# A diffusion transformer's attention layer: weights split on another engine, output sums held in PSUM, the second norm in another order

## The chip, the cores and the metric

The kernel runs on one core of one Trainium2 chip. The metric is the device time of one execution in microseconds (us). A core has engines that run side by side and wait for each other by semaphores: TensorE (PE; its weight loads are listed as PEld), VectorE (DVE), ScalarE (ACT), GpSimd (POOL) and SyncE (SP, which issues most DMAs). Matmuls write to PSUM, which the kernel uses as eight banks of 128 x 512 floats.

## The reference: two layers on 256 tokens and 256 of context

The input is 256 latent tokens on a grid of 4 x 64 and 256 context tokens, 1024 wide. Layer 0 mixes with a retention scan, layer 1 with neighbourhood attention; each has an MLP with a squared ReLU. Cut to layer 1, where the change lies:

```python
h  = x * (1 + sc1) + sh1                    # modulation; hc likewise from ctx
q, k, v = split(h @ w_in)                   # 32 heads of 32
kc, vc  = split((hc @ w_in)[..., d:])       # keys and values of the context
# a query at (row, column) sees all 4 rows, 16 columns around its own, and the context
s = concat([q . k_band * scale + rpb, q . kc * scale])
o = softmax(s) @ [v_band, vc]
y = o @ w_o
x = layer_norm(a * x + g1 * y)              # first norm of the layer
h = x * (1 + sc2) + sh2
x = layer_norm(a * x + g2 * (relu(h @ w1) ** 2) @ w2)
```

All of it is in float32. "The second norm" in the change's name is the modulated norm between attention and MLP: it is the second of the layer's stages that norm and modulate.

## The kernel before

**Products.** A float32 product is made of three faster ones: each operand is split into a rounded part (hi) and the rest (lo), and hi x hi, hi x lo and lo x hi are summed in PSUM (`mm3`, L179).

**Weights.** All weights come as units of 512 KB, in the order of a list (`specs`). `fetch` (L255) issues a unit's DMA on SP into one of 4 raw tiles and has ACT cast it to hi; the subtraction that makes lo is put on a list, and `lows` (L295) issues so many of these on DVE. hi and lo tiles are rings of 5. `take` (L300) hands units to the matmuls. A raw tile is free again when its lo is made.

**Order.** In the part that the change touches each engine runs its instructions in the order in which the program issues them: a wrapper (`InOrder`, L79) pins the order, and it records every instruction with line 89, so the profile's rows are told apart by the names of their tiles, not by lines. PE, ACT and DVE are pinned through the whole attention layer, POOL only from the tail on.

**The attention loop** (L1832 to L1846) has 14 steps. Work is cut into 16 attention units n: four heads (g = n // 2) and half of the queries (n % 2). Step n does, in program order:

- `turned(n)` (L1675): ACT copies the transposed reciprocals of the sums from the bank `pav` to `rt`;
- `scores(n + 2)` (L1591): matmuls into four banks (`pqk`) from `qT` and `kT`;
- `soften(n + 2)` (L1609): for each of four heads, DVE adds the bias to the scores and takes the minimum in one custom instruction (`s<-pqk,bias`, and `mn`; called a biased sum below), then ACT takes the exponential and its sum; at its end POOL issues the DMA of a later unit's bias;
- side work that keeps TensorE busy: a group's keys K(2) to K(7), queries Q(2), Q(3), four blocks of values V(0) to V(3), or blocks of the output projection (W00, W01, W10: first half of the heads' sums for output half and token tile), set by the table `STEPS` (L1811);
- `flip(n + 1)` (L1649): 16 small and 8 larger transposes of the exponentials (`ppt`), copied out by ACT and DVE as a near part and a far part (`pt`), and the transpose of the reciprocals (`pav<-cst,rr`);
- `attend(n)` (L1680): 16 groups of matmuls into `pav`, a product with `rt` on DVE, and its split into `oTh` (ACT) and `oTl` (DVE);
- `invert(n + 2)` (L1637): the reciprocals of the sums and their widening (`rr`), both on DVE.

The five columns of `STEPS` say how many units are fetched and made low ahead of the scores (early), behind the exponentials (late) and behind the flip (last), and which side work runs ahead of the flip and behind attend.

**The tail** (from L1849) does the last two units' attend, the second half of the output projection (`wo_last`, L1863), the gated residual (`gated`, `add_to`), the layer norm's statistics (`stat`, `moments`), the centring of the halves (`center`, tile `xn`), the transposes of these (`pt<-cst,xn`), the affine modulation and its split (`affine_half`: `hTh`, `hTl`), and the first four blocks of the MLP's first product (`tok_block`: p00, p01, p10, p11, tiles `p1t`; the first digit is the token tile). In the tail, before the change, the weight unit that does not fit in the rings lives in scratch tiles.

Of the kernel before, what the change touches and what calls it, by code (L numbers as in the profile page):

```python
# [17 lines left out]
P = 128  # L18
# [74 lines left out]


class Rows:


    def __init__(self, tiles):
        self.tiles = tiles

    def __getitem__(self, at):
        p, k, cols = at
        return self.tiles[k][p, cols]
# [6 lines left out]
def kernel(  # L110
# [144 lines left out]
    def fetch(n, in_scratch=False):  # L255

        for src, k, ncol in specs[len(units) : len(units) + max(n, 0)]:
            raw = rawp.tile([P, k, ncol], F32, tag="raw", name=nm("raw"))
            sp.dma_start(out=raw[:], in_=src.rearrange("(k p) n -> p k n", p=P))
            if in_scratch:  # L260
                hi, lo = Rows([scr("hi", F32R) for _ in range(k)]), Rows([scr("lo", F32R) for _ in range(k)])
                for i in range(k):
                    act.copy(out=hi[:, i, :], in_=raw[:, i, :])
                    pending.append((lo[:, i, :], raw[:, i, :], hi[:, i, :]))
                units.append((hi, lo))
                continue
            hi = hip.tile([P, k, ncol], F32R, tag="hi", name=nm("hi"))
            lo = lop.tile([P, k, ncol], F32R, tag="lo", name=nm("lo"))
# [1380 lines left out]
    def flip(n):  # L1649
# [30 lines left out]
    def attend(n):  # L1680
# [32 lines left out]
    def wo_first(half, t):  # L1713
# [4 lines left out]
        mmo(wops[half, t], t, (0, 1, 2, 3), wous[half])  # L1718
# [70 lines left out]
    flip(0)  # L1789
# [18 lines left out]
    W00, W01, W10, W11 = [W(half, t) for half in range(2) for t in range(2)]  # L1810
# [16 lines left out]

    def run(fs):
        for f in fs:
            f()  # L1830

    for n, (early, late, last, before, after) in enumerate(STEPS):  # L1832
# [27 lines left out]
    x0, x1 = xn2[:, 0, :], xn2[:, 1, :]  # L1860
    st1 = small(smp, 24, "st1", name="st1", bufs=1).rearrange("p (q s) -> p q s", q=4)

    def wo_last(t, half, cols=slice(0, 512)):  # L1863
        ps = bank("pnw")
        mmo(ps, t, (4, 5, 6, 7), us[half::2], cols)
        return ps

    def settle_last(t, half, ps):
        add_to(t, half, gated(ps, t, half, G1), dve)
        if t == 0:  # L1870
            stat(t, half)
# [13 lines left out]
    pool.on = True  # L1885
# [10 lines left out]
    for half in range(2):  # L1896
        center(0, half, mv0, r0, x0, shift)
    settle_last(1, 0, wo_last(1, 0))
    for q in range(2):
        stat_quarter1(q)  # L1900
# [6 lines left out]
    def affine_half(pts, half, t, on_act):  # L1907
# [5 lines left out]
        return lambda: dve.tensor_sub(out=lo, in0=av_, in1=hi.bitcast(F32))  # L1913

    def tok_block(t, f2):
        ps = bank("p1t")
        for k in range(KC):
            wh, wl = us4[2 * f2 + k // 4]
            mm3(
                ps[:, :256], hs(k, t * P, (t + 1) * P), (wh[:, k % 4, :], wl[:, k % 4, :]),  # L1920
                k == 0, k == KC - 1,
            )
# [26 lines left out]
    fetch(2)  # L1949
# [28 lines left out]
    HS1 = [N_Q, N_V, N_B, N_P0, N_P1, N_OH, N_OL, N_K1]  # L1978
# [153 lines left out]
```

## Time and profile before

| | |
|---|---|
| median of 3 runs (lowest, highest) | 1217.92 us (1217.80, 1218.52) |
| the profiled execution | 1219.88 us |
| its span in the trace | 1218.10 us |
| mean granted TensorE clock | 0.992 |
| attention loop from V(0) to V(3), tail, in the trace | about 865 to 990, 990 to 1032 |

Rows of a timeline give start and duration in us, the engine, the operation with its output and input tiles, how many instructions are drawn together (x), and in brackets the idle time ahead of them with what ended it. Rows of groups give total busy time and mean ns of one instruction, then the idle time ahead of them. Rows of the windows view give a stretch, its length, and each engine's busy time in it, then the granted clock of TensorE. Rows of waits give who waits for whom, us in total, how often, and the longest. Durations of matmuls overlap, so the distance of their starts is what counts.

### The profile page before, as it was taken

What the parts mean: (1) busy time and instruction counts of PE and PEld (TensorE: products, weight loads), DVE (VectorE), ACT (ScalarE), POOL (GpSimd) and SP (SyncE); (2) the same over time, 40 slices, a digit from 0 to 9 for tenths busy, and PEclk for the clock granted to TensorE, in tenths of its full rate; (3) what the DMA queues carried; (4) which work ended last, traced back from release to release, by engine and by line L of the source; (5) the groups of instructions that cost most, each with busy time, mean ns of one, the idle gap of its engine ahead of it and who ended that gap; (6) DMA issues with size and microseconds to landing.
All of it is one profiled execution on the core that took longest, in us unless ns stands there. A gap on an engine that the chain in (4) does not pass through costs nothing.

```text
span 1218.1 us, 18130 instructions
## 1 busy us (share of the span) xinstructions
PE 1189.4 (98%) x7138; PEld 991.0 (81%) x7138; DVE 811.0 (67%) x1277; ACT 479.6 (39%) x818; POOL 167.9 (14%) x190
## 2 busy tenths in 40 slices
PE   9999999999999999999999999999999989999996
PEld 6768888888888888888888888888777767999885
DVE  3686766956788476468866664667465677776445
ACT  3652232222323145232213341246465655565331
POOL 0203301420520240000220000230201000000002
PEclk9999999999999999999999999999999989999998
DMA  9665342584255224347665656636543343665661
GB/s 323 214 225 160 121 137 75 160 303 137 93 158 157 80 79 136 92 128 252 196 214 173 215 190 203 200 100 201 169 124 126 120 133 105 193 204 185 225 191 41
DMA packets 134445, 199.15 MB, mean 163 GB/s; under 512 B 15376, under 2 KB 76872, under 8 KB 134360
## 3 DMA queue, kind: packets, MB, share of 16 engines
q1 hardware_dynamic: 129528, 183.86, 47.5%
q0 software_dynamic: 3584, 11.59, 3.1%
q10 hardware_dynamic: 1248, 2.54, 0.7%
q8 instruction: 56, 0.92, 0.3%
q14 instruction: 29, 0.24, 0.1%
HBM read 189.46 MB, written 10.61 MB: 164 GB/s over the span
## 4 chain that ended last, share of the span: by engine, by line
PE 84%; DVE 7%; ACT 5%; DMA 2%; issue 1%; SPq 0%; DVEq 0%; ACTq 0%
PE p L89 41%; PE pg L89 7%; PE pw L89 7%; PE pq L89 6%; PE pv L89 6%; PE pnv L89 3%; PE pn L89 3%; PE po L89 3%; PE pada L89 2%; DVE lo L89 2%; ACT s L89 2%; PE pS L89 1%; ACT hi L89 1%; PE pnw L89 1%; PE ppt L89 1%
## 5 line engine op out<-in xcount | busy, mean ns | idle before, releaser
L89 DVE TENSOR_TENSOR lo<-raw,hi 128x1024 fp32r<-128x1024 f32 (+1 forms) x235 | 276.9, 1193 | 132.8 <-ACT hi L89 132.1
L89 ACT CAST hi<-raw 128x1024 fp32r<-128x1024 f32 (+1 forms) x235 | 234.4, 1011 | 330.9 <-PE p L89 138.8
L89 PE MATMUL p<-hi,hid 128*128 128x512 f32 (+1 forms) x832 | 242.7, 374 | 0.0
L89 PEld LDWEIGHTS p<-hi,hid 128*128 128x128 f32 x832 | 152.2, 188 | 29.1 <-issue 1.6
L89 PE MATMUL p<-hTh,lo 128*128 128x256 f32 (+1 forms) x512 | 168.7, 330 | 0.8 <-DVE lo L89 0.8
L89 PE MATMUL p<-hTh,hi 128*128 128x256 f32 (+1 forms) x512 | 169.1, 331 | 0.0
L89 PE MATMUL p<-hTl,hi 128*128 128x256 f32 (+1 forms) x512 | 168.7, 330 | 0.0
L89 PE MATMUL p<-lo,hid 128*128 128x512 f32 (+1 forms) x416 | 155.3, 373 | 0.0
L89 POOL TENSOR_TENSOR R<-R,acc 128x512 f32<-128x512 f32 x40 | 68.0, 1711 | 277.7 <-DVE acc L89 277.6
L89 PEld LDWEIGHTS p<-hTh,lo 128*128 128x128 f32 x512 | 97.3, 190 | 9.7 <-DVE lo L89 1.0
L89 PEld LDWEIGHTS p<-hTh,hi 128*128 128x128 f32 x512 | 97.2, 190 | 9.6 <-issue 0.8
L89 PEld LDWEIGHTS p<-hTl,hi 128*128 128x128 f32 x512 | 97.3, 190 | 9.0 <-DVE hTl L89 0.4
L89 DVE SCALAR_TENSOR_TENSOR acc<-rawa,scol,acc 128x1024 f32<-128x1024 f32 x56 | 73.9, 1338 | 41.5 <-DMA rawa<-in_ada_w_dram 41.2
L89 PEld LDWEIGHTS p<-lo,hid 128*128 128x128 f32 x416 | 78.4, 188 | 13.4
L89 DVE SCALAR_TENSOR_TENSOR strips<-rawa,scol,strips 128x512 f32<-128x512 f32 x84 | 71.0, 889 | 0.5 <-DMA rawa<-in_ada_w_dram 0.5
L89 ACT CAST hid<-r 128x256 fp32r<-128x256 f32 (+1 forms) x64 | 32.0, 500 | 82.1 <-DVE r L89 82.1
L89 DVE TENSOR_TENSOR hid<-r,hid 128x256 fp32r<-128x256 f32 (+1 forms) x64 | 34.6, 541 | 32.6 <-ACT hid L89 32.4
L89 ACT ACTIVATE s<-s,mn 128x416 f32<-128x416 f32 x64 | 40.4, 633 | 32.5 <-DVE mn L89 32.0
L89 PE MATMUL pg<-hi,hTh 128*128 128x512 f32 x128 | 51.0, 399 | 0.0
L89 PE MATMUL pw<-hi,oh 128*128 128x512 f32 x128 | 51.0, 398 | 0.0
L89 PE MATMUL pv<-hi,hTh 128*128 128x512 f32 x128 | 50.7, 396 | 0.0
L89 PE MATMUL pw<-hi,ol 128*128 128x512 f32 x128 | 50.3, 393 | 0.0
(213 smaller groups left out, 2190.1 us busy)
## 6 DMA issues: line engine op xcount, KB each, us to landing
raw<-in_mlp_w_dram SPq DMA_DIRECT2D x128, 512.0 KB
rawa<-in_ada_w_dram SPq DMA_DIRECT2D x80, 512.0 KB
raw<-in_ret_w_in_dram SPq DMA_DIRECT2D x46, 512.0 KB
raw<-in_nat_w_in_dram SPq DMA_DIRECT2D x24, 512.0 KB
rawq<-in_ada_w_dram SPq DMA_DIRECT2D x16, 512.0 KB
raw<-in_ret_w_o_dram SPq DMA_DIRECT2D x16, 512.0 KB
rpb_near<-far SPq DMA_DIRECT2D x20, 256.0 KB
bias<-rpb_near POOLq DMA_DIRECT2D x16, 320.0 KB, 3.9
```

The costliest lines, as they stand in the source:

```text
L89: r = f(*args, **kwargs)
```

## The change

- `soften` of a step no longer has weight subtractions ahead of its biased sums: those sums are DVE's first work behind the scores. In steps 1 to 9 the subtractions are issued on POOL (`lows(1, pool)`), 13 of them; POOL is pinned in order from the loop's start. In step 0 one is left on DVE, behind the first sum. From step 10 on, one a step is issued on DVE behind the sums.
- `flip` is cut into `flip_near` and `flip_far`. The copies of the near part now come ahead of the evacuation of K or Q, the far part behind it. `attend` comes ahead of `invert`.
- Q(3) runs at the start of step 9 ahead of K(6), and six units are fetched in that step where there were four.
- A unit may live in an arena slot that is idle at that time (`home`), which takes the place of the scratch tiles.
- W01 and W10 are not read out after the heads' first half: their banks are held from step 12 and 13, and the second half is summed on top in the tail. W11 is made in the tail, in halves of 256 columns, over all heads in one bank each. So three products with the gate and three sums into the residual of 512 columns fall away.
- In the tail `flip(15)` and `turned(15)` come directly behind `attend(14)`, `attend(15)` behind the second output block, the first token tile's norm ahead of the second tile's last output blocks; p01 is cut into three pieces with the second tile's transposes between them, and `tok_part` sums the terms by kind, those with the low part of the activations last, in each half of the chunks. `fold` and POOL's other operations stand in the pinned order.

The core of the diff (the table `STEPS` is cut to two rows):

```diff
-    def fetch(n, in_scratch=False):
+    def fetch(n, home=None):
...
+            if home is None:
+                hi = hip.tile([P, k, ncol], F32R, tag="hi", name=nm("hi"))
+                lo = lop.tile([P, k, ncol], F32R, tag="lo", name=nm("lo"))
+            else:
+                both_ = slot(home, [P, 2, k, ncol], F32R, "unit")
+                hi, lo = both_[:, 0], both_[:, 1]
...
-    def lows(n=100):
+    def lows(n=100, eng=None):
         for lo, raw, hi in pending[:n]:
-            dve.tensor_sub(out=lo, in0=raw, in1=hi.bitcast(F32))
+            (eng or dve).tensor_sub(out=lo, in0=raw, in1=hi.bitcast(F32))
...
-    def soften(n):
+    def soften(n, between=lambda: None):
...
+            if j == 0:
+                between()
...
-    def flip(n):
+    def flip_near(n):
...
+    def flip_far(n):
...
-        (1, 1, 0, [V(0)], []),
+        ((None,), (None,), V(0), ()),
...
-        (0, 0, 1, [W01[0]], [W01[1]]),
+        ((), (), W01, (None,)),
...
+    pool.on = True
+
+    def weights(homes, eng=None):
+        for home in homes:
+            fetch(1, home)
+            if eng:
+                lows(1, eng)
+
+    for n, (early, late, before, last) in enumerate(STEPS):
         turned(n)
-        fetch(early)
-        lows(early)
+        weights(early, pool if n else None)
         scores(n + 2)
-        soften(n + 2)
-        fetch(late)
-        lows(late)
-        run(before)
-        flip(n + 1)
+        soften(n + 2, lambda: lows(0 if n else 1))
+        if n > 9:
+            lows(1)
+        weights(late, pool if n < 10 else None)
+        if n == 9:
+            Q(3)()()
+            weights((None, None), pool)
+            fetch(1)
+        evac = before()
+        flip_near(n + 1)
+        if evac:
+            evac()
+        flip_far(n + 1)
+        attend(n)
         invert(n + 2)
-        fetch(last)
-        attend(n)
-        run(after)
-        lows()
+        if n == 10:
+            wo_add(0, 0)
+        weights(last, pool if n < 10 else None)
...
     turned(n - 1)
-    attend(n - 1)
-    flip(n)
-    fetch(1, True)
-    lows()
+    weights((N_Q, N_B))
+    attend(n - 1, lambda: lows(1))
+    flip_near(n)
+    flip_far(n)
+    turned(n)
+    lows(2)
...
-    settle_last(0, 0, wo_last(0, 0))
-    settle_last(0, 1, wo_last(0, 1))
+    ps = wo_last(bank("pnw"), 0, 0, first=True)
+    add_to(0, 0, gated(ps, 0, 0, G1), dve)
+    stat(0, 0)
+    tmp = gated(wo_last(wops[1, 0], 0, 1), 0, 1, G1)
+    attend(n, lambda: add_to(0, 1, tmp, dve))
+    weights((N_P0, N_P1))
+    stat(0, 1)
     mv0, r0 = moments(0)
-    turned(n)
-    attend(n)
-    W11[0]()
-    fetch(2)
-    W11[1]()
-    lows()
...
+    add_to(1, 0, gated(wo_last(wops[0, 1], 1, 0), 1, 0, G1), dve)
...
+    mmo(ps[0], 1, (0, 1, 2, 3), wous[1], halves[0], last=False)
     pts0 = [mod_pt(x0, half) for half in range(2)]
     lo0 = [affine_half(pts0, half, 0, True) for half in range(2)]
-    ps = [wo_last(1, 1, slice(256 * q, 256 * q + 256)) for q in range(2)]
...
+    mmo(ps[1], 1, (0, 1, 2, 3), wous[1], halves[1], last=False)
```

What the instructions' order makes of it, at three places. DVE in step 1, with K(3) beside it, before the change (`lo` are the weight subtractions, `s` and `mn` the biased sums, `kT` the split of K):

```order
L89 TENSOR_TENSOR oTl_6961<-rt_7193,oTh_6960 128x128
L89 TENSOR_TENSOR lo_7326<-raw_7323,hi_7325 128x1024
L89 TENSOR_TENSOR lo_7331<-raw_7328,hi_7330 128x1024
L89 ISA s_7353,mn_7351<-pqk_7335,bias_6884 128x416
L89 ISA mn_7351 128x1
L89 ISA s_7356,mn_7351<-pqk_7336,bias_6884 128x416
L89 ISA mn_7351 128x1
L89 ISA s_7359,mn_7351<-pqk_7337,bias_6884 128x416
L89 ISA mn_7351 128x1
L89 ISA s_7362,mn_7351<-pqk_7338,bias_6884 128x416
L89 ISA mn_7351 128x1
L89 TENSOR_TENSOR kT_7244<-pn_7366,kT_7244 128x4x64
```

The same place on DVE after the change:

```order
L89 COPY rr_7318<-sums_7229 128x128
L89 ISA s_7341,mn_7339<-pqk_7323,bias_6884 128x416
L89 ISA mn_7339 128x1
L89 ISA s_7344,mn_7339<-pqk_7324,bias_6884 128x416
L89 ISA mn_7339 128x1
L89 ISA s_7347,mn_7339<-pqk_7325,bias_6884 128x416
L89 ISA mn_7339 128x1
L89 ISA s_7350,mn_7339<-pqk_7326,bias_6884 128x416
L89 ISA mn_7339 128x1
L89 COPY pt_6957<-ppt_7392 128x256
L89 TENSOR_TENSOR kT_7244<-pn_7366,kT_7244 128x4x64
L89 TENSOR_TENSOR kT_7244<-pn_7366,kT_7244 128x256
```

The two subtractions are gone from DVE (they stand on POOL), and the copy of the near part moved ahead of the split of K. ACT in step 9, with Q(3) and K(6), before the change (`hi` are weight casts, `qT` and `kT` evacuations, `pt` copies of transposes):

```order
L89 CAST hi_8364<-raw_8362 128x1024
L89 CAST hi_8369<-raw_8367 128x1024
L89 ACTIVATE qT_6622<-pn_8374 128x4x64
L89 ACTIVATE qT_6622<-pn_8375 128x4x64
L89 CAST kT_8428<-pn_8429 128x4x64
L89 CAST kT_8428<-pn_8429 128x256
L89 COPY pt_6957<-ppt_8458 128x256
L89 COPY pt_6957<-ppt_8470 128x512
```

The same place on ACT after it:

```order
L89 CAST hi_8364<-raw_8362 128x1024
L89 CAST unit_8370<-raw_8368 128x1024
L89 ACTIVATE qT_6622<-pn_8373 128x4x64
L89 ACTIVATE qT_6622<-pn_8374 128x4x64
L89 CAST hi_8429<-raw_8427 128x1024
L89 CAST hi_8435<-raw_8433 128x1024
L89 CAST hi_8441<-raw_8439 128x1024
L89 COPY pt_6957<-ppt_8470 128x256
L89 CAST kT_8444<-pn_8445 128x4x64
L89 CAST kT_8444<-pn_8445 128x256
L89 COPY pt_6957<-ppt_8486 128x512
```

Three more casts of weights now stand between the evacuation of Q(3) and the near copy, and the near copy stands ahead of K(6)'s evacuation. ACT at the loop's end and the tail's start, behind the last exponential, before the change (`oTh` is the split of attend's product, `rt` the copy of the reciprocals):

```order
L89 ACTIVATE s_8888,sums_8878<-s_8888,mn_8877 128x416
L89 COPY pt_6957<-ppt_8904 128x256
L89 COPY pt_6957<-ppt_8916 128x512
L89 CAST hi_8934<-raw_8932 128x1024
L89 CAST oTh_6960<-rt_8859 128x128
L89 COPY rt_8960<-pav_6959 128x128
L89 CAST oTh_6960<-rt_8960 128x128
```

The same place after it:

```order
L89 ACTIVATE s_8893,sums_8883<-s_8893,mn_8882 128x416
L89 COPY pt_6957<-ppt_8910 128x256
L89 COPY pt_6957<-ppt_8922 128x512
L89 CAST oTh_6960<-rt_8864 128x128
L89 COPY rt_8959<-pav_6959 128x128
L89 CAST unit_8963<-raw_8961 128x1024
L89 CAST unit_8967<-raw_8965 128x1024
L89 CAST oTh_6960<-rt_8959 128x128
```

The weight cast that stood ahead of attend(13)'s split and the copy of the reciprocals is gone; two casts stand behind that copy.

More of the change, by code (lines that the diff above doesn't have):

```diff
@@ L92, in __getattr__ @@
         return call
[L95 to L103, printed above, removed]
 PIN = {"sync"}
@@ L259, in fetch @@
             sp.dma_start(out=raw[:], in_=src.rearrange("(k p) n -> p k n", p=P))
[L260 to L268, printed above, removed]
+            if home is None:
[4 more added lines that the diff above has]
+                hi, lo = both_[:, 0], both_[:, 1]
             act.copy(out=hi[:], in_=raw[:])
@@ L1678, in turned, with attend @@
         act.copy(out=rts[n][:], in_=av_half(n)[:, P:])
-    def attend(n):
+    def attend(n, between=lambda: None):
         g, qt = n // 2, n % 2
@@ L1698, in attend, with mmo @@
         dve.tensor_mul(out=rt[:], in0=po[:, :P], in1=rt[:])
+        between()
         split(rt[:], oTh[:, g, tsl(qt)], oTl[:, g, tsl(qt)])
-    def mmo(ps, t, ks, us, cols=slice(0, 512)):
+    def mmo(ps, t, ks, us, cols=slice(0, 512), first=True, last=True):
         oTh, oTl = oTs[0]
@@ L1707, in mmo, with wo_first @@
                 ps[:, cols], (oTh[:, k, tsl(t)], oTl[:, k, tsl(t)]), (wh[:, k % 2, cols], wl[:, k % 2, cols]),
-                k == ks[0], k == ks[-1],
+                first and k == ks[0], last and k == ks[-1],
             )
     wous, wops = {}, {}
-    def wo_first(half, t):
+    def wo_first(half, t, last=True):
         if t == 0:
@@ L1717, in wo_first @@
         wops[half, t] = bank("pnw")
-        mmo(wops[half, t], t, (0, 1, 2, 3), wous[half])
+        mmo(wops[half, t], t, (0, 1, 2, 3), wous[half], last=last)
     def wo_add(half, t):
@@ L1788 @@
     invert(0)
-    flip(0)
+    flip_near(0)
+    flip_far(0)
     residual(1, xns[1], gb, dve)
@@ L1796, in K, with f @@
     def K(g):
-        return lambda: k_part(g)
+        def f():
+            pb = k_mm(g)
+            return lambda: k_evac(pb, g)
+        return f
     def Q(p):
-        return lambda: q_pair(p)
+        def f():
+            for u in range(2):
+                q_mm(p, u)
+            return lambda: q_evac(p)
+        return f
     def V(t):
         return lambda: v_part(1, t)
-    def W(half, t):
-        return lambda: wo_first(half, t), lambda: wo_add(half, t)
-    W00, W01, W10, W11 = [W(half, t) for half in range(2) for t in range(2)]
+    W00, W01, W10 = lambda: wo_first(0, 0), lambda: wo_first(0, 1, False), lambda: wo_first(1, 0, False)
@@ L1828, in run @@
[L1828 to L1832, printed above, removed]
+        ((None,), (), K(2), ()),
+        ((), (None, None), K(3), ()),
+        ((), (None, None), K(4), ()),
+        ((), (None,), K(5), ()),
+        ((), (None, None), Q(2), ()),
+        ((None,), (None,), V(0), ()),
+        ((), (), V(1), ()),
+        ((), (), V(2), ()),
+        ((), (), V(3), (None, None)),
+        ((), (None, N_V), K(6), ()),
+        ((), (N_K0,), W00, ()),
@@ L1855 @@
+    lows(2)
     us = take(4, 0)
-    xn2 = slot(N_K0, [P, 2, D], F32, "xn")
     gb = slot(N_K1, [P, 2, D], F32, "gb")
@@ L1859, with wo_last @@
     A, B = fold(1, 0, 1, 1)
[L1860 to L1865, printed above, removed]
-        return ps
[L1868 to L1871, printed above, removed]
+    def wo_last(ps, t, half, cols=slice(0, 512), first=False):
+        mmo(ps, t, (4, 5, 6, 7), us[half::2], cols, first)
+        return ps
     def settle_quarter(q, ps):
@@ L1883, in stat_quarter1 @@
             with_eps(st1[:, 0, :])
-    pool.on = True
-    settle_last(0, 0, wo_last(0, 0))
-    settle_last(0, 1, wo_last(0, 1))
-    mv0, r0 = moments(0)
-    turned(n)
-    attend(n)
-    W11[0]()
-    fetch(2)
-    W11[1]()
-    lows()
-    shift = shift_of(mv0, r0)
[L1896 to L1900, printed above, removed]
+    ps = wo_last(bank("pnw"), 0, 0, first=True)
[5 more added lines that the diff above has]
+    stat(0, 1)
+    mv0, r0 = moments(0)
+    shift = shift_of(mv0, r0)
+    center(0, 0, mv0, r0, x0, shift)
+    center(0, 1, mv0, r0, x0)
     ht = slot(N_Q, [P, 4, 2, NLAT], F32R, "hid1")
@@ L1912, in affine_half, with tok_part @@
         act.copy(out=hi, in_=av_)
-        return lambda: dve.tensor_sub(out=lo, in0=av_, in1=hi.bitcast(F32))
+        return lambda e=dve: e.tensor_sub(out=lo, in0=av_, in1=hi.bitcast(F32))
+    def tok_part(ps, t, f2, kh, terms=((0, 0), (0, 1), (1, 0))):
+        for a, b in terms:
+            for k in range(4 * kh, 4 * kh + 4):
+                pe.matmul(
+                    ps[:, :256], lhsT=hs(k, t * P, (t + 1) * P)[a], rhs=us4[2 * f2 + kh][b][:, k % 4, :],
+                    start=k == a == b == 0, stop=k == KC - 1 and a == 1,
+                )
     def tok_block(t, f2):
         ps = bank("p1t")
[L1917 to L1922, printed above, removed]
+        for kh in range(2):
+            tok_part(ps, t, f2, kh)
         return ps
@@ L1938, in turn_block @@
         dve.tensor_sub(out=lo, in0=src, in1=hi.bitcast(F32))
+    add_to(1, 0, gated(wo_last(wops[0, 1], 1, 0), 1, 0, G1), dve)
+    for q in range(2):
+        stat_quarter1(q)
+    lows(1)
+    halves = [slice(256 * q, 256 * q + 256) for q in range(2)]
+    ps = [bank("pnw") for _ in range(2)]
+    mmo(ps[0], 1, (0, 1, 2, 3), wous[1], halves[0], last=False)
     pts0 = [mod_pt(x0, half) for half in range(2)]
     lo0 = [affine_half(pts0, half, 0, True) for half in range(2)]
-    ps = [wo_last(1, 1, slice(256 * q, 256 * q + 256)) for q in range(2)]
-    settle_quarter(2, ps[0])
+    mmo(ps[1], 1, (0, 1, 2, 3), wous[1], halves[1], last=False)
     lo0[0]()
-    settle_quarter(3, ps[1])
+    for q in range(2):
+        settle_quarter(2 + q, wo_last(ps[q], 1, 1, halves[q]))
     stats[1] = st1
@@ L1948 @@
     lo0[1]()
-    fetch(2)
     p00 = tok_block(0, 0)
@@ L1954 @@
     lows(1)
+    us4 += take(2, 0)
+    p01 = bank("p1t")
+    tok_part(p01, 0, 1, 0, ((0, 0), (0, 1)))
     pts1 = [mod_pt(x1, half) for half in range(2)]
-    lows(1)
     lo1 = [affine_half(pts1, half, 1, not half) for half in range(2)]
-    us4 += take(2, 0)
-    p01 = tok_block(0, 1)
+    tok_part(p01, 0, 1, 0, ((1, 0),))
+    tok_part(p01, 0, 1, 1)
     for f in lo1:
@@ L1977 @@
     G2 = load_gate(1, 1, 1)
-    HS1 = [N_Q, N_V, N_B, N_P0, N_P1, N_OH, N_OL, N_K1]
+    HS1 = [N_Q, N_K0, N_B, N_P0, N_P1, N_OH, N_OL, N_K1]
     hid = [ht]
```

17 lines of the change are left out of this document (5 added, 12 removed).

## The prediction

> **What bounds the kernel now.** I read the page first, then the windows view of the stretch that the change touches, then TensorE's waits in it, then the timelines of single steps.
>
> ```profile
> PE 1189.4 (98%) x7138; PEld 991.0 (81%) x7138; DVE 811.0 (67%) x1277; ACT 479.6 (39%) x818; POOL 167.9 (14%) x190
> ...
> core 0: us, PE busy (x) PEld busy (x) DVE busy (x) ACT busy (x) POOL busy (x), PEclk, DMA share, GB/s
> 865.00:930.00 65.00, 63.04 (x620) 49.66 (x618) 41.67 (x112) 40.27 (x103) 6.92 (x10) 1.00 0.45 135
> 930.00:948.00 18.00, 18.00 (x188) 14.03 (x188) 8.10 (x28) 9.23 (x27) 4.25 (x7) 1.00 0.33 108
> 948.00:990.00 42.00, 39.96 (x449) 31.41 (x447) 30.58 (x77) 26.96 (x66) 2.25 (x3) 1.00 0.41 131
> 990.00:1032.00 42.00, 35.72 (x283) 30.05 (x282) 31.27 (x64) 21.49 (x47) 1.90 (x4) 0.88 0.37 114
> 1032.00:1045.00 13.00, 13.00 (x112) 13.00 (x111) 9.11 (x14) 8.95 (x16) 0.00 (x0) 1.00 0.49 147
> ```
>
> TensorE is the bound, so all that this change can win is time in which TensorE waits or runs below full clock, and that lies in three stretches: the steps with K, Q and V(0) beside them (865 to 930), the steps with output units (948 to 990), and the tail up to the second MLP (990 to 1032). From 1032 on it is busy without a gap, and in V(1) to V(3) (930 to 948) too. DVE and ACT are at about two thirds there: not full, but with chains through both that TensorE waits for.
>
> ```profile
> PE pav L89 <- ACT rt L89: 2.6, 1, 2.6
> PE pt L89 <- ACT xn L89: 2.0, 1, 2.0
> PE ppt L89 <- DVE mn L89: 1.4, 2, 0.8
> PE p1t L89 <- DVE hTl L89: 0.8, 2, 0.5
> ...
> 998.90 0.87 PE L89 MATMUL pav<-pt,R 128*32 128x128 f32 x16 [2.61 <-ACT rt L89]
> ...
> 1003.36 0.63 PE L89 MATMUL pnw<-lo,oTh 128*128 128x512 f32 x1
> 1003.79 0.63 PE L89 MATMUL pnw<-hi,oTl 128*128 128x512 f32 x1
> ...
> 1005.51 0.40 PE L89 MATMUL pnw<-lo,oTh 128*128 128x512 f32 x1
> 1005.74 0.39 PE L89 MATMUL pnw<-hi,oTl 128*128 128x512 f32 x1
> ...
> 1014.66 2.35 DVE L89 TENSOR_TENSOR lo<-raw,hi 128x1024 fp32r<-128x1024 f32 x2
> ...
> 1031.62 0.28 PE L89 MATMUL p1t<-hi,hTh 128*128 128x256 f32 x1
> ```
>
> The waits are those of the stretch 948 to 1045. Behind the 2.61 us gap at attend(14) the matmuls start 0.43 us apart, where 2 us later the same ones start 0.23 apart: the gap also brought a stretch at about half speed, from 998.9 to a point between the two pairs of rows, which I put at 5.8 us long: 2.9 us lost. The second wait (2.0 us, transposes of the first normed half) stands behind two weight subtractions on DVE (1014.66, 2.35 us), and some 0.6 us of slow matmuls follow it by the same reading. Idle time in 990 to 1032 is 42.00 - 35.72 = 6.3 us, so the tail's loss is 6.3 + 2.9 + 0.6 = 9.8 us, and at most 6.3 + 0.12 x 42 = 11.3 us. [...]
>
> ```profile
> 880.54 1.25 PEld L89 LDWEIGHTS ppt<-cst,s 64*128 64x128 f32 x16 [0.35 <-DVE mn L89]
> 930.22 1.25 PEld L89 LDWEIGHTS ppt<-cst,s 64*128 64x128 f32 x16 [0.35 <-issue]
> 938.99 1.25 PEld L89 LDWEIGHTS ppt<-cst,s 64*128 64x128 f32 x16 [0.35 <-issue]
> 947.85 1.25 PEld L89 LDWEIGHTS ppt<-cst,s 64*128 64x128 f32 x16 [0.35 <-issue]
> ...
> 894.27 0.48 PEld L89 LDWEIGHTS pqk<-kT,qT 32*128 32x128 f32 x9 [0.54 <-DVE kT L89]
> ...
> 889.89 0.65 ACT L89 ACTIVATE s<-s,mn 128x416 f32<-128x416 f32 x1 [1.99 <-DVE mn L89]
> ...
> 886.99 2.36 DVE L89 TENSOR_TENSOR lo<-raw,hi 128x1024 fp32r<-128x1024 f32 x2 [0.82 <-ACT hi L89]
> ```
>
> In the loop a step without waits takes 8.77 us (930.22 to 938.99; the next 8.86). The five steps between 880.54 and 930.22 take 49.68 us, so 49.68 - 5 x 8.77 = 5.8 us are lost in them. Each loses it alike: two subtractions (886.99) stand ahead of the biased sums, the exps wait for those (889.89), the evacuation of K and the copies of the transposes come behind the exps, and the next scores find their banks late (894.27).
>
> **Biased sums first, subtractions on POOL, near copies ahead of K.** In steps 1 to 6 the 2.36 us leave DVE, and scores then wait for the near copies only. What is late next is the round through ACT and DVE: near copy, K's split, far copy, attend's product and its split, 1/sum, one biased sum, four exps, two casts of weights.
>
> ```profile
> L89 ACT COPY pt<-ppt 128x256 f32<-128x256 f32 (+1 forms) x28 | 12.1, 478 | 0.2
> L89 DVE TENSOR_TENSOR kT<-pn,kT 128x256 fp32r<-128x256 f32 x12 | 5.8, 541 | 11.3 <-ACT kT L89 11.3
> L89 DVE TENSOR_TENSOR rt<-pav,rt 128x128 f32<-128x128 f32 x14 | 4.0, 284 | 0.0
> L89 DVE TENSOR_TENSOR oTl<-rt,oTh 128x128 fp32r<-128x128 f32 x14 | 4.1, 293 | 7.2 <-ACT oTh L89 7.2
> L89 DVE CUSTOM_DVE_ANT_1 s<-pqk,bias 128x416 f32<-128x416 f32 x49 | 26.2, 586 | 1.1 <-DMA bias<-rpb_near 1.1
> L89 ACT ACTIVATE s<-s,mn 128x416 f32<-128x416 f32 x56 | 35.4, 633 | 28.0 <-DVE mn L89 27.5 <-ACT s L89 0.4
> L89 ACT CAST hi<-raw 128x1024 fp32r<-128x1024 f32 x20 | 20.4, 1049 | 0.0
> ```
>
> In that order 2 x 0.48 + 0.54 + 0.28 + 0.29 + 0.59 + 4 x 0.63 + 2 x 1.05 = 7.3 us; for the two casts that stand between (kT, oTh), 1/sum with its widening and the hand-overs I take 1.7 (estimate), together 9.0. That is 0.2 over 8.77, 1.1 us in five steps. To it comes what POOL costs.
>
> ```profile
> 807.07 2.54 POOL L89 TENSOR_TENSOR hTl<-aff,hTh 128x512 fp32r<-128x512 f32 x2 [2.17 <-ACT hTh L89]
> ...
> L89 POOL TENSOR_TENSOR R<-R,acc 128x512 f32<-128x512 f32 x40 | 68.0, 1711 | 277.7 <-DVE acc L89 277.6
> ...
> 242.98 4.43 POOL L89 TENSOR_TENSOR R<-R,acc 128x512 f32<-128x512 f32 x2 [1.23 <-DVE acc L89]
> ...
> 244.56 1.71 DVE L89 TENSOR_TENSOR lo<-raw,hi 128x1024 fp32r<-128x1024 f32 x1
> ...
> L89 POOL DMA_DIRECT2D bias<-rpb_near x12 | 9.1, 758 | 90.7 <-DVE mn L89 90.7
> ```
>
> No row has a 128x1024 subtraction on POOL. The nearest, two of 128x512, take 2.54 us alone (807.07); two beside subtractions on DVE take 4.43 (242.98), and one of DVE's then takes 1.71 instead of 1.18. I take 2.54, since in the loop DVE's work beside it is mostly sums and copies out of PSUM, and charge DVE's short operations with two inputs in SBUF (oTl) and the widening of 1/sum with a wait of 0.35 us a step, 1.9 us in all (estimate; between 0 and 0.53 x 5 = 2.7 by the 244.56 row). [...] The loop's gain is then 5.8 - 1.1 - 1.9 = **2.8 us**, between 0 and 5.8 - 1.1 = 4.7. Bias loads (0.76 us of POOL each) now queue behind the subtractions; a step has room (2 x 2.54 + 0.76 = 5.8 of 8.8).
>
> **Steps 9 to 13.** Here seven units queue on POOL at the end of V(3). Counting from 947.85, with 2.54 each and one bias load, the last unit of K(6) is ready at 12.3, just when its second half is due (12), W00's at 17.4 (due 18), so these cost nothing; W00's wait for its low part (0.8 us of the idle 2.04 here) goes. New is the sixth unit fetched in step 9: its raw tile comes free at 12.3 and needs a transfer.
>
> ```profile
> 1035.00 0.37 SPq L89 DMA_DIRECT2D raw<-in_mlp_w_dram  x1
> ...
> 1038.83 1.05 ACT L89 CAST hi<-raw 128x1024 fp32r<-128x1024 f32 x1 [1.41 <-DMA raw<-in_mlp_w_dram]
> ...
> 1028.86 5.82 PE p1t L89 x48
> ```
>
> With 3.8 us for that (1035.00 to 1038.83) its cast on ACT runs from 16.1 to 17.2. Behind it, in ACT's order, stand K(6)'s near copy and K's split, for which scores(12) wait: about 1.5 us late. The waits for DVE's sums inside the transposes go, but with two of the eight PSUM banks held from step 12 on, scores(13) and scores(15) wait about 1 us each for a near copy behind exps and a cast. I put these together at 4.0 us by starts of matmuls against 3.5 us by the same count now: **0.5 us lost**, between 2 lost and 1.0 won. The merged accumulations (three products and sums over 512 columns fewer) are off TensorE's path, since DVE is busy 30.58 of 42: nothing.
>
> **The tail.** attend(14)'s wait shrinks: the sums stand directly behind scores(15), no subtraction (1.2 us, half of the 1014.66 row) and no accumulation ahead of them, so 1.2 us instead of 2.6 remain (estimate), and no slow stretch follows. Four output blocks, attend(15) and a quarter block then stand ahead of the first transposes of the normed half, some 10 us of matmuls, so the 2.0 us go; p00 and p01 order their terms so that the low parts come later, so the 0.8 us go. The last block as 24 matmuls of 256 columns costs 24 x 0.121 (5.82 / 48) = 2.9 us against 12 x 0.23 = 2.8: 0.1. Of 9.8 us, 1.2 stay, and the longer gaps between groups that the idle time doesn't count add some 0.4: gain 9.8 - 1.2 - 0.1 + 0.5 = **9.0 us**, at most 11.3 - 1.2 + 0.1 = 10.2. The first block p10, which starts at 1031.62 now, is where this ends; nothing behind it changes but where the tiles lie.
>
> Sum: 2.8 - 0.5 + 9.0 = 11.3 us. The profiled execution took 1219.88 us (span 1218.10 and 1.78 around it), 1.96 above the median; it would come to 1208.6, and the median of 1217.92 to **1206.6 us**.
>
> **The rivals.** B: POOL's subtractions hold DVE's short operations up to a whole subtraction, and the loop gains nothing: 1217.92 - 8.5 = 1209.4. For it stands the 1.71 of the 244.56 row, against it that such DVE operations are few (0.3 us each). C: the tail's first wait stays at 2.6 because ACT still comes late to its copy of the reciprocals (exps, copies and a cast of weights stand ahead of it), and the slow stretch comes again: 1.4 + 2.9 = 4.3 us worse, 1210.9. D, slower: POOL becomes the bound. At twice 2.54, 5.1 us a unit (a little over the 4.43 of the 242.98 row), the nine units up to V(0) with five bias loads take 9 x 5.1 + 5 x 0.76 = 49.7 us against 5 x 8.8 = 44 of steps: 5.7 late; K(6)'s last unit, third in POOL's queue from 3.8 on, comes at 3.8 + 15.3 + 0.8 = 19.9 instead of 12: 8 late. With the tail's 9.0 won: 1217.92 + 5.7 + 8 - 9.0 = 1222.6. The point where it turns is about 4.75 us a unit. Against it: only neighbours with two large SBUF inputs brought 4.43. E, no effect: the held banks and late casts give back what the tail wins, about 1218.
>
> **How the numbers follow.** Forecast 0.62, B 0.17, C 0.10, E 0.04, D 0.07. The bounds of the terms give 4.7 + 1.0 + 10.2 = 15.9 us at best, 1202.0; on the other side the range reaches past B and C to 1212, which leaves out D, E and the far ends. The runs of before lie within 0.06%; 0.2% (2.4 us) is what a measurement can tell. Faster by more: 0.62 + 0.17 + 0.10 = 0.89, of which I move 0.01 to each side: 0.87; same 0.05; slower 0.08.
>
> **What would show it.** Right: transposes in steps 1 to 6 about 9.2 to 9.4 us apart; POOL's 128x1024 subtractions near 2.54 us; a TensorE wait under 1.5 us at attend(14) and a granted clock of 1.00 through the tail; p10 starting some 11 us earlier. Wrong: subtractions on POOL of over 4 us, TensorE waiting for lo from POOL in V(0) or K(6) (D); a clock under 0.95 in the tail (C); steps still 9.9 us apart (B).

## The result, and the profile after

| | before | after |
|---|---|---|
| median of 5 runs (lowest, highest) | 1217.80 us (1217.34, 1218.52) | 1206.79 us (1203.88, 1208.19) |
| the profiled execution | 1219.88 us | 1206.79 us |
| its span | 1218.10 us | 1205.0 us |

The ratio is 0.9904, with a 95% interval of 0.989 to 0.9917. The medians lie 11.0 us apart, where 1206.6 us and 11.3 us were forecast. The sum held; two of its three terms did not, and that their errors cancelled was luck. To see that, the span is cut at four starts on TensorE: the transposes of step 0, those behind V(3), W10's first matmul, and the first matmul of the MLP's second block (tile `p`). The last two of these in the profile before, and then in the profile after, there with the transposes of the first steps ahead of them:

```profile
990.05 0.50 PE L89 MATMUL pnw<-hi,oTh 128*128 128x512 f32 x1
...
1037.97 0.36 PE L89 MATMUL p<-hTh,hi 128*128 128x256 f32 x1
```

```profile
873.31 1.25 PEld L89 LDWEIGHTS ppt<-cst,s 64*128 64x128 f32 x16 [0.35 <-issue]
882.07 1.25 PEld L89 LDWEIGHTS ppt<-cst,s 64*128 64x128 f32 x16 [0.35 <-issue]
890.93 1.25 PEld L89 LDWEIGHTS ppt<-cst,s 64*128 64x128 f32 x16 [0.35 <-issue]
899.70 1.25 PEld L89 LDWEIGHTS ppt<-cst,s 64*128 64x128 f32 x16 [0.35 <-issue]
...
987.18 0.50 PE L89 MATMUL pnw<-hi,oTh 128*128 128x512 f32 x1
...
1024.88 0.36 PE L89 MATMUL p<-hTh,hi 128*128 128x256 f32 x1
```

By these starts, with the same cuts in every kernel's trace (all in us; the last three rows are taken up below):

| profile | up to the loop | loop to V(3) | to W10 | W10 to `p` | rest of the span |
|---|---|---|---|---|---|
| before | 871.8 | 76.1 | 42.2 | 47.9 | 180.1 |
| after | 873.3 | 70.9 | 43.0 | 37.7 | 180.1 |
| before, again (two) | 874.0, 874.0 | 76.0, 76.0 | 42.2, 42.2 | 44.4, 44.4 | 180.1, 180.1 |
| after, again | 873.3 | 70.9 | 42.9 | 37.7 | 180.1 |

The steps up to V(3) are 8.75 to 8.90 us long (one 9.16), where five of them took 9.6 to 10.1. The part ahead of the loop, which the change does not touch, came out 1.5 us later in the profile after; over all the profiles here it lies between 871.8 and 875.5. TensorE's waits of the profile after, from 860 to 1035, and its windows:

```profile
PE pqk L89 <- ACT kT L89: 1.4, 1, 1.4
PE pav L89 <- ACT rt L89: 1.0, 1, 1.0
PE pqk L89 <- DVE kT L89: 0.5, 1, 0.5
PE pn L89 <- POOL lo L89: 0.2, 1, 0.2
...
core 0: us, PE busy (x) PEld busy (x) DVE busy (x) ACT busy (x) POOL busy (x), PEclk, DMA share, GB/s
865.00:930.00 65.00, 65.00 (x688) 51.96 (x688) 35.31 (x108) 42.44 (x108) 28.84 (x20) 1.00 0.49 150
948.00:990.00 42.00, 39.93 (x397) 31.84 (x395) 25.69 (x77) 29.39 (x71) 17.00 (x12) 0.96 0.46 146
990.00:1020.00 30.00, 29.02 (x292) 25.94 (x292) 24.64 (x48) 16.96 (x37) 1.90 (x4) 1.00 0.47 147
```

Nothing waits in 865 to 930. In the tail only attend(14)'s 1.0 us is left. The waits on K's split (1.4 + 0.5 us) are those of scores(12), ahead of step 10's output block, and the clock of 0.96 shows that a slow stretch now lies in that part.

### The profile page after: what moved, and what is told of

Same layout as the page of the kernel before. It is cut to its first block, busy times and chain, and to the rows that moved or that the text cites. A ratio compares the mean times of both kernels' runs of the same rounds, so it can differ in the third digit from the quotient of the medians.

```text
span 1205.0 us, 18136 instructions
## 1 busy us (share of the span) xinstructions
PE 1182.4 (98%) x7150; PEld 987.8 (82%) x7150; DVE 793.7 (66%) x1256; ACT 480.2 (40%) x816; POOL 203.1 (17%) x205
## 3 DMA queue, kind: packets, MB, share of 16 engines
q10 hardware_dynamic: 1248, 2.54, 0.7%
## 4 chain that ended last, share of the span: by engine, by line
PE 86%; DVE 5%; DMA 4%; ACT 2%; issue 2%; POOL 1%; SPq 0%; DVEq 0%; POOLq 0%; ACTq 0%
PE p L89 42%; PE pg L89 7%; PE pw L89 6%; PE pq L89 6%; PE pv L89 5%; PE pn L89 4%; PE pnv L89 3%; PE po L89 3%; PE pnw L89 2%; DMA rawq<-in_ada_w_dram 2%; PE pada L89 2%; PE ppt L89 1%; PE pS L89 1%; DVE lo L89 1%; PE p1t L89 1%
## 5 line engine op out<-in xcount | busy, mean ns | idle before, releaser
L89 ACT CAST hi<-raw 128x1024 fp32r<-128x1024 f32 (+1 forms) x228 | 228.6, 1013 | 339.8 <-PE p L89 137.7
L89 DVE TENSOR_TENSOR lo<-raw,hi 128x1024 fp32r<-128x1024 f32 (+1 forms) x214 | 253.3, 1195 | 116.7 <-ACT hi L89 114.9
L89 DVE SCALAR_TENSOR_TENSOR strips<-rawa,scol,strips 128x512 f32<-128x512 f32 x84 | 70.9, 886 | 0.9 <-DMA rawa<-in_ada_w_dram 0.9
L89 PE MATMUL pg<-lo,hTh 128*128 128x512 f32 x128 | 50.0, 391 | 0.0
```

The costliest lines, as they stand in the source:

```text
L89: r = f(*args, **kwargs)
```

## The experiments

### Again: how usual was the profiled execution?

The kernel before and the changed kernel, unaltered. Expected of the first two:

> The kernel before, profiled again. Theory (the profiled execution of before was a long one, by the length of its slow stretches in the tail, and a usual one has less): the loop (76.1 us) and steps 9 to 12 (42.2) come out the same within 0.2 us, and the stretch from W10's first matmul to the second MLP block is 43 to 46 us where it was 47.9. Rival (the tail always takes 47.9 and the difference lies in layer 0): 47.5 to 48.2.

> The same once more, with the same numbers expected: 43 to 46 us, against 47.5 to 48.2 for the rival.

Both gave 44.4 us in the tail, not 47.9, with the loop and steps 9 to 12 unchanged. The first of them, at attend(14) and behind it, and its window over the tail:

```profile
1001.10 0.54 PE L89 MATMUL pav<-pt,R 128*32 128x128 f32 x16 [2.61 <-ACT rt L89]
...
1004.33 0.39 PE L89 MATMUL pnw<-lo,oTh 128*128 128x512 f32 x1
1004.55 0.39 PE L89 MATMUL pnw<-hi,oTl 128*128 128x512 f32 x1
...
990.00:1032.00 42.00, 34.74 (x336) 28.67 (x329) 33.64 (x72) 24.99 (x56) 1.90 (x4) 1.00 0.43 136
```

The gap is the same 2.61 us, yet the matmuls behind it start 0.22 us apart and the clock stays at 1.00: this gap is followed by the slow stretch in some executions and not in others. How often is open: the kernel `b_pool_lows` below leaves the tail as it was, and its profile has slow matmuls behind the gap again and 46.6 us from W10 to `p`:

```profile
990.00:1032.00 42.00, 35.74 (x303) 31.02 (x302) 32.61 (x65) 23.44 (x48) 1.91 (x4) 0.92 0.38 119
```

So two of four profiles with this tail are clean (44.4 us), and the first one (47.9) is the slowest. What decides between the two, no run here shows. The changed kernel once more:

> The changed kernel, profiled again. Theory (the slow stretch behind scores(12) comes in some executions only, its waits of 1.4 and 0.5 us in all of them): the loop takes 70.9 us and the tail 37.7 as before, steps 9 to 12 take 43.0 us with a slow stretch (clock under 0.95 from 948 to 990) or about 42.0 without. Rival (steps 9 to 12 take 43.0 whatever the clock): 43.0 with a clock of 1.00.

It showed the slow stretch again (clock 0.96, 42.9 us, waits of 1.2 and 0.5 us), so this run does not tell the two apart. The kernel `a_no_hold` below does: it has the same waits (1.5 and 0.5), takes 42.0 us there, and its window has a clock of 1.00. By that difference the slow stretch is worth 1.0 us.

```profile
948.00:990.00 42.00, 39.82 (x423) 31.58 (x426) 26.50 (x76) 28.96 (x72) 16.39 (x12) 1.00 0.48 158
```

### The subtractions on DVE again

```diff
-        weights(early, pool if n else None)
+        weights(early, dve if n else None)
...
-        weights(late, pool if n < 10 else None)
+        weights(late, dve if n < 10 else None)
...
-            weights((None, None), pool)
+            weights((None, None), dve)
...
-        weights(last, pool if n < 10 else None)
+        weights(last, dve if n < 10 else None)
```

> The changed kernel with the weight subtractions of steps 1 to 9 on DVE instead of POOL, at the same places of the program, so that two stand ahead of the biased sums again. Theory (the loop's 5.2 us come from the subtractions that no longer stand ahead of the sums): steps 1 to 5 take about 9.9 us again where two subtractions stand, and the time is 1206.8 + 5 = about 1212. Rival (the gain came from the near copies ahead of K's split, which is kept here): steps stay near 8.8 us and the time at about 1207.

Measured: 1206.29 us, a ratio of 0.9898 (0.9886 to 0.9911), no slower than the changed kernel. The steps lie between the two forecasts:

```profile
881.77 1.25 PEld L89 LDWEIGHTS ppt<-cst,s 64*128 64x128 f32 x16 [0.35 <-issue]
890.89 1.25 PEld L89 LDWEIGHTS ppt<-cst,s 64*128 64x128 f32 x16 [0.35 <-issue]
900.25 1.25 PEld L89 LDWEIGHTS ppt<-cst,s 64*128 64x128 f32 x16 [0.35 <-issue]
```

They take 9.1 and 9.4 us (9.1 to 9.8 over the five), and the loop 73.1: with subtractions ahead of the sums, 3.0 of the 5.2 us stay won, by the rest of the loop's new order (near copies ahead of K's split, attend ahead of 1/sum; these two were not tried apart). That the time is nevertheless the same is due to steps 9 to 12, 40.6 us here against 43.0: scores(12) wait 0.5 + 0.5 us instead of 1.4 + 0.5, and no slow stretch follows (clock 1.00). So POOL wins 2.2 us in the loop, and 2.4 are given back behind it: 0.9 of wait, 1.0 of slow stretch, and 0.5 that are not accounted for.

Both waits stand behind the cast of the last unit that step 9 fetches. Two rows each of the chain that leads to that cast (start, us, what), for the changed kernel and for this one:

```profile
953.88 2.43 POOL lo L89
956.32 4.62 DMA raw<-in_nat_w_o_dram
...
956.71 1.24 DVE lo L89
957.96 3.57 DMA raw<-in_nat_w_o_dram
```

The subtraction frees the unit's raw tile 12.1 us behind the start of V(3)'s transposes on POOL (956.3) and 11.9 us on DVE (957.95): nearly the same, though one takes 2.4 us and the other 1.2. What differs by 1.0 us is the transfer into that tile. With POOL it starts 3.1 us after the transfer before it (953.18), with DVE 5.4 (952.60); why it is the longer one with POOL is not shown.

The same with the early units' subtractions behind the sums:

```diff
-        weights(early, pool if n else None)
+        weights(early)
...
         if n > 9:
             lows(1)
+        elif n:
+            lows()
...
-        weights(late, pool if n < 10 else None)
+        weights(late, dve if n < 10 else None)
```

> The changed kernel with the subtractions of steps 1 to 9 on DVE, those of the early units behind the four biased sums. Theory A (only the order on DVE counts, DVE has room): steps stay at 8.8 to 9.0 us, 1207 to 1208. Theory B (POOL is needed: 2.4 us of subtractions behind the sums now delay the near copy, K's split and attend's product on DVE): steps of 9.5 us or more, 1210 to 1213.

Measured: 1205.46 us (0.9881 to 0.9908), loop 72.6, steps 9 to 12 40.6. The steps take 9.1 to 9.6 us, between the two theories, and the time is below both. Theory B has the mechanism: behind the sums the subtractions cost nearly what they cost ahead of them (72.6 against 73.1), so they cost on DVE at both places that were tried.

### The subtractions on POOL alone

```diff
-        lows(early)
+        lows(early, pool if 0 < n < 10 else None)
...
-        lows(late)
+        lows(late, pool if n < 10 else None)
```

This is the kernel before with POOL's order pinned from the loop's start and these two lines.

> The kernel before with one part of the change alone: the subtractions of steps 1 to 9 on POOL, everything else as it was (K's split ahead of the near copies, all of the tail). Theory (the sums ahead are what counts): the loop gains nearly all of its 5.2 us, 1217.8 - 5 = about 1213. Rival (without the near copies ahead of K's split the scores still wait for their banks): steps of about 9.4 us, a gain of 2 to 3 us, about 1215.5.

Measured: 1213.60 us (9 runs), a ratio of 0.9965 (0.9951 to 0.9978), 4.3 us. The steps:

```profile
874.45 1.25 PEld L89 LDWEIGHTS ppt<-cst,s 64*128 64x128 f32 x16 [0.35 <-issue]
883.22 1.25 PEld L89 LDWEIGHTS ppt<-cst,s 64*128 64x128 f32 x16 [0.35 <-issue]
892.11 1.25 PEld L89 LDWEIGHTS ppt<-cst,s 64*128 64x128 f32 x16 [0.35 <-issue]
```

The loop takes 70.9 us, as in the changed kernel: this one part wins all of its 5.2 us, and the new order of copies, which wins 3.0 without it, adds nothing to it. The rival is refuted.

### What holds up scores(12)

By the table `STEPS`, step 9 of the changed kernel fetches five units, not six, and POOL makes 15 subtractions in steps 1 to 9, not 13; the unit called the sixth is the last of the five. Its cast on ACT comes late, and the near copy of step 9 and K(6)'s split stand behind it:

```profile
961.02 1.04 ACT L89 CAST hi<-raw 128x1024 fp32r<-128x1024 f32 x1 [1.89 <-POOL lo L89]
961.97 0.36 ACT L89 COPY pt<-ppt 128x256 f32<-128x256 f32 x1
962.23 0.83 ACT L89 CAST kT<-pn 128x256 fp32r<-128x256 f32 x2
...
962.90 0.35 PE L89 MATMUL pqk<-kT,qT 32*128 32x160 f32 x4 [1.36 <-ACT kT L89]
963.76 0.92 PE L89 MATMUL pqk<-kT,qT 32*128 32x160 f32 x20 [0.51 <-DVE kT L89]
...
966.90 0.63 PE L89 MATMUL pnw<-unit,oTl 128*128 128x512 f32 x1
967.33 0.63 PE L89 MATMUL pnw<-hi,oTh 128*128 128x512 f32 x1
```

The first row names POOL, where a subtraction of another unit ended at that moment. By the rows of the chain above, the cast waited for its transfer, which ended at 960.94; in `a_again` the row of the same cast says so:

```profile
960.83 1.05 ACT L89 CAST hi<-raw 128x1024 fp32r<-128x1024 f32 x1 [1.17 <-DMA raw<-in_nat_w_o_dram]
```

The last two rows of the first fence, 0.43 us apart, are the slow stretch. The edit moves the fetch:

```diff
             weights((None, None), pool)
-            fetch(1)
...
         flip_far(n + 1)
+        if n == 9:
+            fetch(1)
         attend(n)
```

> The changed kernel with one edit: the sixth unit of step 9 is fetched behind the far copies of that step. Theory (the cast of that unit on ACT holds scores(12) up and the gap of 1.4 + 0.5 us brings a slow stretch): the cast no longer stands ahead of the near copy, scores(12) wait under 0.5 us, the granted clock is 1.00 from 948 to 990, and the time falls by 2.5 us of waits and some 1.5 us of the slow stretch, to about 1203. Rival (scores(12) wait for K(6)'s split, whatever stands ahead of it, or the unit then comes late for W10): the wait moves to another place and the time stays at 1206 to 1207.

Measured: 1203.52 us (1203.18 to 1204.19, 4 runs), a ratio of 0.9875 (0.9863 to 0.9888). Steps 9 to 12 take 39.9 us, and the wait is gone:

```profile
961.00 0.96 PE L89 MATMUL pqk<-kT,qT 32*128 32x160 f32 x24
...
948.00:990.00 42.00, 40.63 (x446) 32.33 (x448) 27.82 (x81) 31.19 (x78) 16.98 (x12) 1.00 0.53 169
```

The theory holds: 3.1 us off that stretch. This is the fastest kernel of the study, 3.3 us below the changed one.

### What the tail's gain is made of

First, W01's accumulation moved behind the sums of step 13, in the kernel before:

```diff
         soften(n + 2)
+        if n == 13:
+            W01[1]()
...
-        run(after)
+        if n != 12:
+            run(after)
```

> The kernel before with one edit: the product with the gate and the sum into the residual for W01 (1.4 us on DVE) stand behind the biased sums of step 13 instead of ahead of them; the weight subtraction stays ahead. Theory (attend(14)'s gap is the chain sums, exps, copies, reciprocals behind what DVE does first, and the slow stretch comes from the gap's length): the gap falls from 2.6 to 1.2 us, no slow stretch follows, the time falls by 1.4 + 2.9 = 4.3 us, a ratio of about 0.9965 to the kernel before. Rival (the slow stretch comes with any gap, or the gap is another's): 1.4 us at most, a ratio of 0.9988 or more.

Measured: a ratio of 1.000 (0.9989 to 1.0012). The gap is 2.3 us where it was 2.6, and slow matmuls follow it in this profile (clock 0.92 from 990 to 1032). The theory is refuted on size, and the time is the rival's. The accumulation only moved along the same chain, from ahead of the sums to ahead of the copies and of 1/sum, so this run does not test what the gap's length does.

Second, the shift ahead of the two subtractions:

```diff
     W11[1]()
-    lows()
     shift = shift_of(mv0, r0)
     for half in range(2):
         center(0, half, mv0, r0, x0, shift)
+    lows()
```

> The kernel before with one edit in the tail: the two weight subtractions (2.35 us on DVE) stand behind the shift that the centring of the first token tile waits for, not ahead of it. Theory: the wait of 2.0 us ahead of the transposes of the normed half goes, with 0.6 us of slow matmuls behind it: 2.6 us, a ratio of about 0.998. Rival (the 2.35 us come back at the first tile's low parts or at the second tile's statistics, which DVE does next): the wait moves, within 0.5 us of the kernel before.

Measured: a ratio of 0.9994 (0.9985 to 1.0003). The wait of 2.0 us is gone from the trace, and the wait for the low parts of the activations grew from 0.8 to 1.4 us. That leaves 1.4 us, within the interval's reach of 1.8; the other 0.6 us forecast were slow matmuls, which the clean executions above do not have. By the medians (0.5 us) this is nearer to the rival.

Third, three moves together, the last fetch of step 13 among them:

```diff
-        fetch(last)
+        if n != 13:
+            fetch(last)
         attend(n)
-        run(after)
+        if n != 12:
+            run(after)
+        if n == 13:
+            W01[1]()
...
     flip(n)
+    fetch(1)
     fetch(1, True)
...
     W11[1]()
-    lows()
     shift = shift_of(mv0, r0)
...
         center(0, half, mv0, r0, x0, shift)
+    lows()
```

> The kernel before with three things moved and nothing else of the change: W01's product and sum into the residual behind attend(13), the last fetch of step 13 (a cast of 1.05 us on ACT) behind attend(14) and the transposes of unit 15, and the two weight subtractions behind the shift. Theory (the tail's gain is order alone: what stands ahead of the exps, of the copy of the reciprocals and of the shift): attend(14)'s gap falls under 1.5 us, the 2.0 us ahead of the normed half's transposes go, the stretch from W10's first matmul to the second MLP block takes about 40 us, where the changed kernel has 37.7, and the ratio to the kernel before is about 0.9965. Rival (the held banks and the new order of the blocks are needed): 42.5 us or more, a ratio of 0.998 or more.

Measured: 1215.12 us, a ratio of 0.9973 (0.9962 to 0.9983), 42.4 us for the stretch. TensorE's waits from 950 to 1045:

```profile
PE pnw L89 <- DVE lo L89: 1.5, 2, 0.8
PE p1t L89 <- DVE hTl L89: 1.4, 2, 0.9
PE pav L89 <- ACT rt L89: 1.3, 1, 1.3
PE pav L89 <- DVE rt L89: 0.7, 1, 0.7
PE ppt L89 <- DVE mn L89: 0.7, 1, 0.7
PE pqk L89 <- ACT pt L89: 0.4, 1, 0.4
PE pnw L89 <- ACT hi L89: 0.3, 1, 0.3
```

The two gaps are gone or halved, as the theory has it, but the work put off comes back: the weight unit is late for the first output block, the activations' low parts for p00. Of the 6.7 us between 44.4 and 37.7 these moves win 2.0. The rest comes with the new order of the blocks, which puts more matmuls between cause and use, and with the held banks; the order was not tried by itself. That is nearer to the rival.

Fourth, the changed kernel without held banks:

```diff
-lambda: wo_first(0, 1, False), lambda: wo_first(1, 0, False)
+lambda: wo_first(0, 1), lambda: wo_first(1, 0)
...
+        if n == 12:
+            wo_add(0, 1)
+        if n == 13:
+            wo_add(1, 0)
...
-    tmp = gated(wo_last(wops[1, 0], 0, 1), 0, 1, G1)
+    tmp = gated(wo_last(bank("pnw"), 0, 1, first=True), 0, 1, G1)
...
-    add_to(1, 0, gated(wo_last(wops[0, 1], 1, 0), 1, 0, G1), dve)
+    add_to(1, 0, gated(wo_last(bank("pnw"), 1, 0, first=True), 1, 0, G1), dve)
```

> The changed kernel with W01 and W10 read out in steps 12 and 13 as before the change (product with the gate and sum into the residual on DVE behind 1/sum of that step) and their second halves summed in banks of their own in the tail. Theory (held banks win by keeping 1.4 us off DVE ahead of the last sums): attend(14)'s gap grows from 1.0 to 2.4 us, a slow stretch follows, about 4 us slower than the changed kernel: 1210 to 1211. Rival (DVE has room, it is the order that wins): the gap stays under 1.3 us and the time at 1206 to 1207.

Measured: 1205.66 us (0.9888 to 0.9914); attend(14)'s gap is 1.4 us and the tail 38.2. Nearer to the rival: the held banks win 0.5 us in the tail, and in the time nothing that can be told.

Fifth, the fetch moved as above, and the reciprocals' copy for attend(14) put forward:

```diff
+        if n == 13:
+            turned(n + 1)
         attend(n)
...
-    turned(n - 1)
     weights((N_Q, N_B))
```

> The changed kernel with the sixth unit of step 9 fetched behind the far copies, and with the copy of the reciprocals for attend(14) on ACT ahead of attend(13)'s split in step 13 instead of behind it. Theory (attend(14) waits for that copy only because it stands behind a split that waits for DVE's product): the gap of 1.0 us goes, and the time falls from 1203.5 to 1202.5. Rival (the copies of the far part end no sooner than that): the gap stays at 0.7 or more, 1203.2 to 1203.5.

Measured: 1204.26 us (1202.66 to 1206.84), a ratio of 0.9891 (0.9877 to 0.9905), the tail 37.6 us. Its waits, from 950 to 1045:

```profile
PE pav L89 <- DVE rt L89: 0.5, 1, 0.5
PE pav L89 <- ACT rt L89: 0.4, 1, 0.4
```

The gap of 1.0 us became 0.4 ahead of attend(13), which now waits for that copy, and 0.5 ahead of attend(14), for attend(13)'s product. That is nearer to the rival: 0.9 us of wait remain, and the tail takes what it took (37.6 against 37.7). What sets the wait was not taken apart further.

## Why the prediction was right or wrong

**The loop (2.8 us forecast, 5.2 measured, outside the bounds of 0 to 4.7).** The direction was right, the size not. Two charges were made that TensorE never paid. The round through ACT and DVE was put at 9.0 us, "0.2 over 8.77, 1.1 us in five steps"; the rows of the profile after have it longer still where two units are cast, 9.4 us from one near copy to the next, and 8.5 in the step behind, where one is:

```profile
882.68 0.36 ACT L89 COPY pt<-ppt 128x256 f32<-128x256 f32 x1
...
892.09 0.36 ACT L89 COPY pt<-ppt 128x256 f32<-128x256 f32 x1
...
900.56 0.36 ACT L89 COPY pt<-ppt 128x256 f32<-128x256 f32 x1
```

But a round that is 0.6 us longer than the step cost nothing here, where there was room ahead of the scores: TensorE has no wait from 865 to 930, since the long round used the room up and the step with one unit gave it back. The prediction had charged each step in full. The other charge was POOL's (1.9 us; five waits of 0.35 are 1.75). The wait is there, in the groups of 870 to 945 and in one step:

```profile
L89 DVE TENSOR_TENSOR oTl<-rt,oTh 128x128 fp32r<-128x128 f32 x8 | 4.0, 500 | 2.9 <-ACT oTh L89 2.9
L89 DVE TENSOR_TENSOR kT<-pn,kT 128x256 fp32r<-128x256 f32 x8 | 3.9, 534 | 3.9 <-ACT kT L89 3.9
...
891.33 4.73 POOL L89 TENSOR_TENSOR lo<-raw,hi 128x1024 fp32r<-128x1024 f32 x2 [1.08 <-ACT hi L89]
...
895.36 0.85 DVE L89 TENSOR_TENSOR oTl<-rt,oTh 128x128 fp32r<-128x128 f32 x1 [0.37 <-ACT oTh L89]
```

The operation with two inputs in SBUF takes 0.85 us instead of 0.29 and ends just behind POOL's second subtraction (891.33 + 4.73 = 896.06); the one that reads PSUM keeps its 0.53. Of the eight such operations there three are that long (0.82 to 0.86 us), each beside a subtraction on POOL, and the others keep 0.29. That cost 8 x (0.50 - 0.29) = 1.7 us on DVE, and none on TensorE. No run shows DVE held up for a whole subtraction of POOL in a step, on which the lower bound of 0 and rival B stand: the longest of these operations lost 0.86 - 0.29 = 0.57 us. POOL's subtraction was sized well: 2.4 us against 2.54.

**Steps 9 to 13 (0.5 us lost forecast, 0.8 measured).** The wait at scores(12) was forecast at 1.5 us for the reason that the moved fetch then confirmed; it was 1.4 + 0.5. Behind V(3)'s transposes the raw tile came free at 12.1 us and the cast started at 16.8, where 12.3 and 16.1 were forecast; six subtractions queue on POOL there, as the times of the forecast count, and not seven. What was missed is the slow stretch behind it, 1.0 us. The waits of 1 us at scores(13) and scores(15) did not come.

**The tail (9.0 us forecast; 6.7 measured against a clean execution, 10.2 against the first profile).** The waits went as forecast: 1.0 us of the first gap stayed (1.2 forecast), the other two went, and no slow stretch came (clock 1.00 from 990 to 1032). The step that failed is "9.8 us" for the loss now: 3.5 of it were slow matmuls, and the two executions profiled again have none, so their tail takes 44.4 us and not 47.9. One execution was taken for all: the prediction saw that it lay 1.96 us above the median, and yet took the whole gain off the median too. Without the slow matmuls its sum is 6.3 - 1.2 - 0.1 + 0.5 = 5.5 us (the 0.5 stand as "some 0.4" in its text), where 6.7 were measured. Against the first execution the gain is 10.2 us, which is why the profiles differ by 13.1 us in span, in spite of 1.5 us lost ahead of the loop, where the medians differ by 11.0. The reason given for the shorter gap was also weaker than it looked: the accumulations taken off DVE were worth 0.5 us, and moving them alone won nothing.

**The sum** was 2.8 - 0.5 + 9.0 = 11.3. Against clean executions of the tail it is 5.2 - 0.8 + 6.7 = 11.1, and against the first profile 5.2 - 0.8 + 10.2 = 14.6. An underrated loop and a tail taken from one execution with slow matmuls made a total that fits the medians. That it fits within 0.3 us is luck: the part ahead of the loop alone differs by up to 3.7 us between the profiles.

**The rivals.** B (the loop gains nothing by POOL's hold on DVE) is refuted by `b_pool_lows`. D (POOL as the bound) would have needed 4.75 us a unit; it was 2.4. C named the right mechanism in the wrong place: a slow stretch did follow a wait behind a late ACT (clock 0.72 from 962 to 968), at scores(12) instead of attend(14). E (no effect) is refuted by the interval of the ratio.

## What to carry to other kernels

Compare the stretches of two profiles before summing: cut the span at matmuls that both kernels have, and profile the kernel more than once, since a slow stretch behind a gap may belong to some executions alone: behind the gap of 2.6 us the clock from 1000 to 1005 was 0.50 in one execution of the kernel before, and 1.00 in two. A chain that was longer than its step (9.4 us against 8.8) cost nothing here while there was room ahead of its user. What one stretch wins the next can give back: here a cast in front of the near copy cost 3.1 us, where the loop had won 5.2. Where a row names what ended a wait, follow the chain as well: the row of that cast named POOL, the chain a transfer.

## What the runs showed of the hardware

A TensorE gap of 2.6 us at attend(14) was followed by a slow stretch in three profiles (clock from 1000 to 1005: 0.50 in the kernel before, 0.87 in `b_pool_lows`, 0.66 in `b_lows_behind`) and by none in two (the kernel before, again: 1.00 in both); one of 2.3 us (`b_add_behind`) was followed by one (0.73). Gaps of 1.2 to 1.4 and 0.5 us a little apart were followed by one in two profiles of the changed kernel (0.96 from 948 to 990 in both), and gaps of 1.5 and 0.5 us by none in `a_no_hold` (1.00). A gap of 1.0 us at attend(14) was followed by none in five profiles (1.00 from 990 to 1020 in four; in the fifth, `a_again`, W10 to `p` took the same 37.7 us). A subtraction of 128x1024 took 2.4 us on POOL and 1.2 on DVE. Of the DVE operations `oTl<-rt,oTh` (128x128, both inputs in SBUF) those beside a subtraction on POOL took 0.82 to 0.86 us, the others 0.29.
